# Attention scores of two heads on the two halves of TensorE's rows

## The chip, the core and the metric

The kernel runs on one core of a Trainium2 chip. The metric is the device time of one execution in microseconds. Before the change it is 956.52 us, the median of three runs (956.5 to 957.92).

## What is computed

A decoder trunk of two layers on a sequence of 512 tokens and 1024 channels: a pooling mixer and a squared-ReLU MLP, then stick-breaking attention and a second MLP, with RMSNorms around each. All data is float32. The change touches the attention, which has 16 heads of 64 channels:

```python
def stick_breaking_attention(q, k, v):
    for i in range(S // Q_BLOCK):            # blocks of 128 queries
        kv_len = (i + 1) * Q_BLOCK
        z = einsum('bhqd,bhkd->bhqk', q_blk, k_blk) * inv_sqrt_d
        mask = s_idx < t_idx
        log1m = where(mask, -softplus(z), 0.0)
        excl = cumsum(log1m, axis=3, reverse=True) - log1m
        a = where(mask, exp(log_sigmoid(z) + excl), 0.0)
        outs.append(einsum('bhqk,bhkd->bhqd', a, v_blk))
```

## The kernel before

**Precision.** Products of float32 values are made from rounded parts (type fp32r): every operand is split into a high part, a rounded copy made by ScalarE (ACT), and a low part, the rest, made by a subtraction on VectorE (DVE). A product is high x high + high x low + low x high. In most of the kernel these are three matmuls into one PSUM bank (`mm3`, `up_block`).

**Stages.** The pooling layer, the first MLP, the attention stage, the second MLP. The attention stage handles heads in eight pairs, since the 128 columns of one projection are two heads of 64. Its steps are written out in `ATT_ORDER`: P projects keys and queries of a pair (`queries_keys`, 48 matmuls), S makes its scores and weights (`weights`), T turns the weights by transposes (`transposed`, L1023, 20 per pair), A multiplies them with the values (`mix_pair`, L1040), V projects values and O projects the output. Between S and T of one pair stands the projection P of the next. A scheduler decides the final order within each engine from its own simulation, except for the last pair: there the steps are listed by hand in `END_ORDER` and keep that order on every engine ("z" are scores, "x" and "y" the two sigmoids, "sc" the scan, "mu" the product, "T" the transposes).

**Scores before.** Of a pair's projection, partitions 0 to 63 belong to head 0 and 64 to 127 to head 1. `queries_keys` gives each head tiles of its own. Its q tile has the high part on its own half of the partitions and the low part on the other half; its k tile has the high part on both halves. So one matmul over all 128 rows sums high x high and low x high. A third tile, `kl`, has the low part of k on the own half and zeros on the other (set once on POOL, L918), and a second matmul adds high x low. Per pair this takes six copies on ACT (L925, L926, L935) and four subtractions on DVE (L927, L936), each on 64 partitions and 512 columns.

`Head.scores` (L979, L980) makes the scores of one head in three PSUM banks: 128 queries against 512 keys, 128 against 384, and one bank with 128 against 256 twice. The last of these needs only 128 keys but is made 256 wide. That is 2 x 4 matmuls per head and 16 per pair.

**After the scores.** `against` (L988) writes sigmoid(-z) into `u`, and `for_` (L1000) writes sigmoid(z) into `w`, both on ACT. `scan` (L1004) is one DVE scan over all 1280 columns of a head; `weigh` (L1010) multiplies its result into `w`. Then `turn` transposes `w` on TensorE into PSUM, `high` (L1029, ACT) and `low` (L1033, DVE) split the transposed weights, and `products` multiplies them with the values.

PSUM has eight banks of 128 x 512, all from one pool (`ps`).

Of the kernel before, what the change touches and what calls it, by code (L numbers as in the profile page):

```python
# [10 lines left out]
F32 = mybir.dt.float32  # L11
F32R = mybir.dt.float32r
ACT = mybir.ActivationFunctionType
ALU = mybir.AluOpType

P = 128
# [16 lines left out]
TS = [slice(t * P, (t + 1) * P) for t in range(T)]  # L33
# [3 lines left out]
SEG = {3: (0, 512), 2: (512, 384), 1: (896, 256), 0: (1152, 128)}  # L37
# [33 lines left out]

END_ORDER = [
    (w if w.startswith("d7") else w.rstrip("0123456789"), [int(c) for c in w if c.isdigit() and not w.startswith("d7")])
    for w in """D6 R0 R1 z01 z00 x01 z02 x00 z11 x02 z12 y02 sc0 A60 y01 y00 x11 z10 oc60 A61 y11 x10 od60 E01 y10
    mu0 oc61 x12 E00 y12 od61 sc1 T00 hh6 T02 T01 ah00 O00 ah02 d7h ah01 O01 hl6 al02 F01 mu1 E11 ov01
    T11 al00 T10 ah11 al01 F11 ah10 al11 T12 A70 al10 ah12 d7l al12 ov00 A71 oc70 od70 O10 oc71 od71 F00
    ov10 hh7 O11 hl7 G01 ov11 G00 ev01 G11 ev00 s01 E10 ev11 s00 g01 s11 F10 V0 g00 G10 a01 O20 a00 S01
# [13 lines left out]
def trunk(ctx, tc, x, consts, grow, pw, wup, wdn, wq, wk, wv, wo, out):  # L91
    nc = tc.nc
# [11 lines left out]
    def name(s):  # L104
        uid[0] += 1
        return f"{s}{uid[0]}"

    def ps():
        return psum.tile([P, 512], F32, tag="ps", name=name("ps"))
# [29 lines left out]
    behind, latest = {}, {}  # L139
# [81 lines left out]
    def make():  # L221
        k, src, scaled = queue.pop(0)
        if k in kept:
            made[k] = place(k)
            for n, t in enumerate(made[k]):
                latest["sp"] = nc.sync.dma_start(t.bitcast(F32), kept[k][n])
            return
        made[k] = weight(src, place(k), scaled)

    def fill(n=1):  # L230
        if gate[0]:
            behind.update(latest)
        for _ in range(n):
            if queue and len(made) < ahead and (queue[0][0][0] != "dn" or dn_pool[0]):
                make()

    def get(key):
        while key not in made:
            make()
        return made.pop(key)  # L240

    for l in range(2):
        if l == 1:
            n = len(queue)
# [176 lines left out]
    def need(*tiles):  # L421
        for t in tiles:
            if t in pending:
                pending.pop(t).transpose()
# [67 lines left out]
    def y_tiles():  # L492
        return [work.tile([P, D], F32, tag=f"y{t}", name=name(f"y{t}")) for t in range(T)]
# [207 lines left out]
    def up_block(pu, w, cols):  # L701
        wh = w[0].rearrange("p (k c) -> p k c", k=KC)
        wl = w[1].rearrange("p (k c) -> p k c", k=KC)
        for k in range(KC):
            nc.tensor.matmul(pu[:, cols], wh[:, k, :], xnh[:, k, cols], start=k == 0, stop=False)  # L705
            nc.tensor.matmul(pu[:, cols], wh[:, k, :], xnl[:, k, cols], start=False, stop=False)  # L706
            nc.tensor.matmul(pu[:, cols], wl[:, k, :], xnh[:, k, cols], start=False, stop=k == KC - 1)  # L707


    with tc.tile_pool(name="mix0", bufs=1, reuse_waits="tile") as mp:  # L710
# [29 lines left out]
        left, stats, ups, ys, own = {}, {}, {}, {}, {}  # L740
# [128 lines left out]
    with tc.tile_pool(name="att", bufs=1, reuse_waits="tile") as ap:  # L869
# [30 lines left out]
        def project(key):  # L900
            need(*range(T))
            if key in started:
                pq, w = started.pop(key)
                up_block(pq, w, slice(S // 2, S))
            else:
                pq = ps()
                up_block(pq, get(key), slice(0, S))
            return pq

        def qk_tile(tag):  # L910
            return ap.tile([P, S], F32R, tag=tag, name=name(tag))

        half = [slice(0, HD), slice(HD, P)]


        kls = [qk_tile(f"kl{a}") for a in range(2)]
        for a in range(2):
            nc.gpsimd.memset(kls[a][half[1 - a], :].bitcast(F32), 0.0)  # L918

        def queries_keys(p):  # L920
            qs, ks = [], []
            pk = project(("k", p))
            for a in range(2):
                k, kl, own, other = qk_tile(f"k{a}"), kls[a], half[a], half[1 - a]
                nc.scalar.copy(k[own, :], pk[own, :])  # L925
                latest["act"] = nc.scalar.copy(k[other, :], pk[own, :])  # L926
                latest["dve"] = nc.vector.tensor_tensor(  # L927
                    out=kl[own, :], in0=pk[own, :], in1=k[own, :].bitcast(F32), op=ALU.subtract
                )
                ks.append(k)  # L930
            fill()
            pq = project(("q", p))
            for a in range(2):
                q, own, other = qk_tile(f"q{a}"), half[a], half[1 - a]
                latest["act"] = nc.scalar.copy(q[own, :], pq[own, :])  # L935
                latest["dve"] = nc.vector.tensor_tensor(  # L936
                    out=q[other, :], in0=pq[own, :], in1=q[own, :].bitcast(F32), op=ALU.subtract
                )
                qs.append(q)
            fill()  # L940
            return qs, ks

        begin = ap.tile([P, NSEG], mybir.dt.bfloat16, tag="begin", name="begin")
        nc.gpsimd.memset(begin, 0.0)
# [1 line left out]
        for lo, n in SEG.values():  # L949
# [3 lines left out]
                out=d, in_=d, pattern=[[-1, P + c]], base=c - 1, channel_multiplier=1,  # L953
# [6 lines left out]
        class Head:  # L960
# [9 lines left out]
                self.qk, self.p, self.a, self.u = qk, p, a, us[a]  # L970
                self.pz, self.pt, self.parts, self.to = {}, {}, {}, {}

            def scores(self, b):
                q, k, kl = self.qk[0][self.a], self.qk[1][self.a], kls[self.a]
                pz = self.pz[b] = ps()
                o = 0
                for i in self.SCORES[b][0]:
                    n = max(256, (i + 1) * P)
                    nc.tensor.matmul(pz[:, o : o + n], q[:, TS[i]], k[:, :n], start=True, stop=False)  # L979
                    nc.tensor.matmul(pz[:, o : o + n], q[:, TS[i]], kl[:, :n], start=False, stop=True)  # L980
                    o += n

            def against(self, b):
                tiles, at = self.SCORES[b]
# [64 lines left out]
            def out(self, o):  # L1049
                own = half[self.a]  # L1050
                nc.vector.tensor_tensor(out=o[own, :], in0=self.po[half[0], :], in1=o[own, :], op=ALU.add)

        def weights(p):
            hs = [Head(qk[p], p, a) for a in range(2)]
            for x in hs:
                for b in range(3):
                    x.scores(b)
                    x.against(b)
                    x.for_(b)
                x.scan()  # L1060
                x.weigh()
            return hs
# [27 lines left out]
        vs, os, wos, y = {}, {}, {}, y_tiles()  # L1090
# [6 lines left out]
        def end():  # L1097

            p, last = PAIRS - 2, PAIRS - 1
            heads[last] = [Head(qk[last], last, a) for a in range(2)]  # L1100
            w = {c: get(("o", c)) for c in range(2, 6)}
            bank, o, ups, up = {}, {}, {}, {}
# [66 lines left out]
            def half_up(j):  # L1169
# [2 lines left out]

            last_heads = heads[last]
            steps = {
                "z": lambda a, b: last_heads[a].scores(b), "x": lambda a, b: last_heads[a].against(b),
                "y": lambda a, b: last_heads[a].for_(b), "sc": lambda a: last_heads[a].scan(),
                "mu": lambda a: last_heads[a].weigh(), "T": lambda a, b: last_heads[a].turn(b),
                "ah": lambda a, b: last_heads[a].high(b), "al": lambda a, b: last_heads[a].low(b),
# [24 lines left out]
        for what, i, part in ATT_ORDER:  # L1203
            if what == "V":
                values(i, part)
            elif what == "K":
                start(("k", i))
            elif what == "P":
                qk[i] = queries_keys(i)
                if i == PAIRS - 1:  # L1210
                    until(("o", 5))
            elif what == "S":
                gate[0] = True
                heads[i] = weights(i)
                fill()
            elif what == "T":
                transposed(heads[i])
                behind.update(latest)
            elif what == "A":
                mix_pair(i, vs[i // 2][1])  # L1220
            elif what == "O" and part:
                out_proj(i, part)
                if i == 0:
                    with tc.issue_after(latest["sp"].ins):
                        gpost1 = gain_row(R_MIX_POST1)
            elif what == "E":
                end()
# [58 lines left out]
```

## Time and profile before

| | |
|---|---|
| median of three runs | 956.52 us (956.5 to 957.92) |
| profiled execution, span | 955.0 us |
| instructions | 12510 |
| TensorE matmuls (PE) busy | 940.7 us, 4757 of them |
| weight loads (PEld) busy | 799.6 us |
| VectorE (DVE) busy | 707.1 us |
| ScalarE (ACT) busy | 576.6 us |
| GpSimd (POOL) busy | 44.7 us |
| TensorE clock granted | 0.997 of full speed |

The profiled execution is one run beside the three timed ones; the profile gives its span from the first to the last instruction. In the profile, PE is the matmuls and PEld the weight loads, which overlap them. A group's row gives line, engine, operation, tiles written and read, shape and count, then busy microseconds and the mean nanoseconds of one, then idle time of the engine before it and what ended it. Matmuls are pipelined: one of 512 columns is shown with 0.39 us while the next starts sooner, so start-to-start times are what counts for TensorE. A row of the timeline is start, duration, engine, line, operation, tiles.

### The profile page before, as it was taken

The numbers are of one execution on the slowest core, as the hardware profiler recorded it, in microseconds if no ns is written. First come the engines' busy times: TensorE is split into PE (matmuls) and PEld (weight loads), VectorE is DVE, ScalarE is ACT, GpSimd is POOL, SyncE is SP. The second block draws the span as 40 slices with busy tenths as digits, with TensorE's granted clock in tenths as the row PEclk, the third lists the DMA queues.
The fourth block names the chain that finished last, engine by engine and source line by source line (L and its number), as shares of the span: only waits on it lengthen the run. The fifth ranks groups of instructions, "written<-read, shape, count | busy, mean of one in ns | idle before, by whom it ended". The sixth has DMA issues, their size and how long they took to land.

```text
span 955.0 us, 12510 instructions
## 1 busy us (share of the span) xinstructions
PE 940.7 (98%) x4757; PEld 799.6 (84%) x4758; DVE 707.1 (74%) x810; ACT 576.6 (60%) x1015; POOL 44.7 (5%) x88
## 2 busy tenths in 40 slices
PE   9999999999999999999999999999999999999996
PEld 6998888888888878999899988898888888888885
DVE  5875799988979866476577778874595966957856
ACT  6667979788775646456656554775545544444632
POOL 2300000000000004000000000300000000000002
PEclk9999999999999999999999999999999999999998
DMA  8244969789697750422434271342513233133102
GB/s 307 99 175 151 338 216 359 293 282 343 221 326 266 273 192 2 179 88 88 162 125 171 95 265 45 127 139 68 197 39 129 97 132 110 45 132 110 47 21 88
DMA packets 43261, 156.14 MB, mean 163 GB/s; under 512 B 4289, under 2 KB 4673, under 8 KB 43202
## 3 DMA queue, kind: packets, MB, share of 16 engines
q1 hardware_dynamic: 43202, 155.36, 45.4%
q8 instruction: 37, 0.61, 0.3%
q14 instruction: 22, 0.18, 0.1%
HBM read 121.79 MB, written 33.55 MB: 163 GB/s over the span
## 4 chain that ended last, share of the span: by engine, by line
PE 86%; DVE 4%; ACT 3%; POOL 3%; DMA 2%; issue 1%; SPq 0%; POOLq 0%; DVEq 0%; ACTq 0%
PE ps L587 27%; PE ps L707 15%; PE ps L705 15%; PE ps L706 15%; PE ps L284 2%; PE ps L285 2%; PE ps L286 2%; PE ps L1040 2%; ACT xn L269 2%; PE ps L819 1%; PE ps L1023 1%; POOL stat L273 1%; DVE x L333 1%; PE ps L979 1%; POOL stat L280 1%
## 5 line engine op out<-in xcount | busy, mean ns | idle before, releaser
L587 PE MATMUL ps<-w,a 128*128 128x512 f32 x1176 | 278.6, 389 | 0.0
L707 PE MATMUL ps<-xnh,w 128*128 128x512 f32 (+1 forms) x712 | 261.6, 368 | 0.1
L706 PE MATMUL ps<-xnl,w 128*128 128x512 f32 (+1 forms) x712 | 261.5, 368 | 0.0
L705 PE MATMUL ps<-xnh,w 128*128 128x512 f32 (+1 forms) x712 | 261.2, 368 | 0.0
L587 PEld LDWEIGHTS ps<-w,a 128*128 128x128 f32 x1176 | 220.7, 188 | 45.9 <-DVE w L266 0.2
L707 PEld LDWEIGHTS ps<-xnh,w 128*128 128x128 f32 x712 | 134.2, 188 | 22.4 <-DVE w L840 0.3
L706 PEld LDWEIGHTS ps<-xnl,w 128*128 128x128 f32 x712 | 134.2, 189 | 21.8
L705 PEld LDWEIGHTS ps<-xnh,w 128*128 128x128 f32 x712 | 133.7, 189 | 22.1
L596 DVE TENSOR_TENSOR y<-ps,y 128x512 f32<-128x512 f32 x124 | 84.4, 686 | 42.0 <-PE ps L587 41.8
L156 DVE TENSOR_TENSOR w<-raw,w 128x1024 fp32r<-128x1024 f32 x58 | 70.9, 1222 | 57.7 <-ACT w L154 57.5
L154 ACT CAST w<-raw 128x1024 fp32r<-128x1024 f32 x58 | 61.0, 1051 | 80.5 <-PE ps L707 80.5
L265 ACT CAST a<-r 128x768 fp32r<-128x768 f32 (+1 forms) x60 | 47.6, 794 | 72.4 <-PE ps L587 54.6
L266 DVE TENSOR_TENSOR a<-r,a 128x768 fp32r<-128x768 f32 (+1 forms) x60 | 54.0, 900 | 11.8 <-ACT a L265 11.6
L265 ACT CAST w<-e 128x1536 fp32r<-128x1536 f32 (+1 forms) x30 | 41.8, 1395 | 25.6 <-DVE e L561 16.2
L1004 DVE TENSOR_TENSOR_SCAN e<-u,begin 128x1280 f32<-128x1280 f32 x16 | 45.2, 2822 | 11.3 <-ACT u L988 10.4
L266 DVE TENSOR_TENSOR w<-e,w 128x1536 fp32r<-128x1536 f32 (+1 forms) x30 | 49.4, 1647 | 1.8 <-ACT w L265 1.6
L165 ACT ACTIVATE apart<-apart,eye 128x128 f32<-128x128 f32 (+1 forms) x132 | 43.1, 407 | 0.2 <-DMA apart<-in_wk 0.2
L266 DVE TENSOR_TENSOR w<-w,w 128x1536 fp32r<-128x1536 f32 (+1 forms) x20 | 33.0, 1649 | 8.1 <-ACT w L265 8.1
L619 ACT ACTIVATE r<-ps 128x512 f32<-128x512 f32 x56 | 33.0, 589 | 8.3 <-PE ps L707 8.2
L284 PE MATMUL ps<-w,xnh 128*128 128x256 f32 x128 | 36.6, 286 | 1.4 <-ACT xnh L395 1.4
L266 DVE TENSOR_TENSOR w<-xn,w 128x1536 fp32r<-128x1536 f32 (+1 forms) x20 | 33.0, 1650 | 5.6 <-ACT w L265 5.5
L620 ACT ACTIVATE r<-r 128x512 f32<-128x512 f32 x56 | 35.5, 633 | 1.3
(131 smaller groups left out, 1394.7 us busy)
## 6 DMA issues: line engine op xcount, KB each, us to landing
raw<-in_wup SPq DMA_DIRECT2D x64, 512.0 KB, 3.8
w<-kept SPq DMA_DIRECT2D x60, 512.0 KB, 4.1
kept<-wx SPq DMA_DIRECT2D x30, 512.0 KB, 4.9
w<-in_wdn SPq DMA_DIRECT2D x8, 1536.0 KB, 7.7
kept<-apart SPq DMA_DIRECT2D x24, 512.0 KB, 5.1
xn<-in_wdn SPq DMA_DIRECT2D x8, 1536.0 KB, 8.2
raw<-in_wdn SPq DMA_DIRECT2D x8, 512.0 KB, 3.5
apart<-in_wk SPq DMA_DIRECT2D x7, 512.0 KB, 6.4
```

Source lines behind the costliest of these rows:

```text
L154: nc.scalar.copy(hi, raw)
L156: nc.vector.tensor_tensor(out=lo, in0=raw, in1=hi.bitcast(F32), op=ALU.subtract)
L165: nc.scalar.mul(c, c, gc[:, lo + k : lo + k + 1])
L265: latest["act"] = nc.scalar.copy(hi, src)
L266: latest["dve"] = nc.vector.tensor_tensor(out=lo, in0=src, in1=hi.bitcast(F32), op=ALU.subtract)
L284: nc.tensor.matmul(dst, ah, bh, start=start, stop=False)
L587: nc.tensor.matmul(bank, a[:, x, q, TS[t]], w[:, z, q], start=start and q == 0 and k == 0, stop=q == self.n - 1 and k == 2, skip_group_che ...
L596: nc.vector.tensor_tensor(out=part, in0=bank, in1=part, op=ALU.add)
L705: nc.tensor.matmul(pu[:, cols], wh[:, k, :], xnh[:, k, cols], start=k == 0, stop=False)
L706: nc.tensor.matmul(pu[:, cols], wh[:, k, :], xnl[:, k, cols], start=False, stop=False)
L707: nc.tensor.matmul(pu[:, cols], wl[:, k, :], xnh[:, k, cols], start=False, stop=k == KC - 1)
L1004: nc.vector.tensor_tensor_scan(out=self.e[:, ::-1], data0=self.u[:, 1:][:, ::-1], data1=begin[:, ::-1], initial=0.0, op0=ALU.mult, op1=ALU ...
```

## The change

Both heads of a pair share four tiles: high and low of k, high and low of q, each over all 128 partitions. That takes two copies and two subtractions per pair, each on 128 partitions. Each score block is now three matmuls over 64 rows per head (high x high, high x low, low x high). The head on the lower half of the partitions uses rows 0 to 63 of the array, the other rows 64 to 127, and the matmuls of the two heads alternate. They write different PSUM banks. The last block is 128 wide. A pair has 24 score matmuls. The scores of both heads now come before the sigmoids in the program, bank by bank, and in the hand-written order of the last pair the steps z1, z0, z2 stand for both heads.

```diff
-    for w in """D6 R0 R1 z01 z00 x01 z02 x00 z11 x02 z12 y02 sc0 A60 y01 y00 x11 z10 oc60 A61 y11 x10 od60 E01 y10
+    for w in """D6 R0 R1 z1 z0 x01 z2 x00 x02 y02 sc0 A60 y01 y00 x11 oc60 A61 y11 x10 od60 E01 y10
...
-        kls = [qk_tile(f"kl{a}") for a in range(2)]
-        for a in range(2):
-            nc.gpsimd.memset(kls[a][half[1 - a], :].bitcast(F32), 0.0)
-
         def queries_keys(p):
-            qs, ks = [], []
-            pk = project(("k", p))
-            for a in range(2):
-                k, kl, own, other = qk_tile(f"k{a}"), kls[a], half[a], half[1 - a]
-                nc.scalar.copy(k[own, :], pk[own, :])
-                latest["act"] = nc.scalar.copy(k[other, :], pk[own, :])
-                latest["dve"] = nc.vector.tensor_tensor(
-                    out=kl[own, :], in0=pk[own, :], in1=k[own, :].bitcast(F32), op=ALU.subtract
-                )
-                ks.append(k)
-            fill()
-            pq = project(("q", p))
-            for a in range(2):
-                q, own, other = qk_tile(f"q{a}"), half[a], half[1 - a]
-                latest["act"] = nc.scalar.copy(q[own, :], pq[own, :])
-                latest["dve"] = nc.vector.tensor_tensor(
-                    out=q[other, :], in0=pq[own, :], in1=q[own, :].bitcast(F32), op=ALU.subtract
-                )
-                qs.append(q)
-            fill()
-            return qs, ks
+            both = []
+            for what in "kq":
+                src = project((what, p))
+                hi, lo = qk_tile(f"{what}h"), qk_tile(f"{what}l")
+                latest["act"] = nc.scalar.copy(hi, src)
+                latest["dve"] = nc.vector.tensor_tensor(out=lo, in0=src, in1=hi.bitcast(F32), op=ALU.subtract)
+                both.append((hi, lo))
+                fill()
+            return both
...
-            def scores(self, b):
-                q, k, kl = self.qk[0][self.a], self.qk[1][self.a], kls[self.a]
-                pz = self.pz[b] = ps()
-                o = 0
-                for i in self.SCORES[b][0]:
-                    n = max(256, (i + 1) * P)
-                    nc.tensor.matmul(pz[:, o : o + n], q[:, TS[i]], k[:, :n], start=True, stop=False)
-                    nc.tensor.matmul(pz[:, o : o + n], q[:, TS[i]], kl[:, :n], start=False, stop=True)
-                    o += n
...
+        def scores(hs, b):
+            (kh, kl), (qh, ql) = hs[0].qk
+            for x in hs:
+                x.pz[b] = ps()
+            o = 0
+            for i in Head.SCORES[b][0]:
+                n = SEG[i][1]
+                for m, (x, y) in enumerate(((qh, kh), (qh, kl), (ql, kh))):
+                    for h in hs:
+                        own = half[h.a]
+                        nc.tensor.matmul(
+                            h.pz[b][:, o : o + n], x[own, TS[i]], y[own, :n], start=m == 0, stop=m == 2,
+                        )
+                o += n
...
             hs = [Head(qk[p], p, a) for a in range(2)]
+            for b in range(3):
+                scores(hs, b)
             for x in hs:
                 for b in range(3):
-                    x.scores(b)
                     x.against(b)
                     x.for_(b)
...
-                "z": lambda a, b: last_heads[a].scores(b), "x": lambda a, b: last_heads[a].against(b),
+                "z": lambda b: scores(last_heads, b), "x": lambda a, b: last_heads[a].against(b),
```

## Prediction

> **What bounds the kernel now.** I read the page's totals first, then the attention stage (about 385 to 587 us) by windows and waits, then the timeline of single instructions inside it.
>
> ```profile
> span 955.0 us, 12510 instructions
> ...
> PE 940.7 (98%) x4757; PEld 799.6 (84%) x4758; DVE 707.1 (74%) x810; ACT 576.6 (60%) x1015; POOL 44.7 (5%) x88
> ```
>
> Matmul busy is modelled, so the 98% alone proves little. The window and the waits of the stage do:
>
> ```profile
> core 0: us, PE busy (x) PEld busy (x) DVE busy (x) ACT busy (x) POOL busy (x), PEclk, DMA share, GB/s
> 430.00:450.00 20.00, 20.00 (x132) 18.40 (x131) 12.30 (x17) 13.03 (x28) 0.00 (x0) 1.00 0.27 102
> ```
>
> ```profile
> PEld ps L979 <- PE ps L980: 0.6, 1, 0.6
> ...
> PE ps L979 <- DVE q L936: 0.4, 1, 0.4
> ```
>
> From 390 to 575 us these are the longest waits of the matmul side: one event, before the last pair's scores. DVE and ACT are busy for under two thirds of the window. So TensorE sets the time here, and a microsecond of scores saved or added moves the end by a microsecond, unless it is eaten at the few places where TensorE has almost caught up with VectorE. The span is one execution; the median of the three times, 956.52, is 1.5 us above it, and I add the change in span to the median.
>
> **The scores before.** The first pair, both heads, on TensorE (start, duration):
>
> ```profile
> 396.58 0.39 PE L979 MATMUL ps<-k,q 128*128 128x512 f32 x1
> 396.81 0.40 PE L980 MATMUL ps<-kl,q 128*128 128x512 f32 x1
> 397.04 0.34 PE L979 MATMUL ps<-k,q 128*128 128x384 f32 x1
> 397.22 0.34 PE L980 MATMUL ps<-kl,q 128*128 128x384 f32 x1
> 397.39 0.28 PE L979 MATMUL ps<-k,q 128*128 128x256 f32 x1
> 397.51 0.28 PE L980 MATMUL ps<-kl,q 128*128 128x256 f32 x1
> 397.62 0.28 PE L979 MATMUL ps<-k,q 128*128 128x256 f32 x1
> ...
> 399.14 0.40 PE L705 MATMUL ps<-xnh,w 128*128 128x512 f32 x1
> ```
>
> What counts is start to start: 0.23 us for 512 columns, 0.175 for 384, 0.12 for 256. Sixteen matmuls take 399.14 - 396.58 = 2.56 us; eight pairs, 20.5 us. That is all the change has to work on.
>
> **The scores after.** Twenty-four matmuls of 64 rows, alternately for the head on the lower and the upper rows; the built program does place them at rows 0 and 64. Nothing in this trace runs on half the rows, so three prices are unknown: whether two matmuls run at once, whether their weight loads do, and what a change between 128-row and 64-row matmuls costs. For a narrow matmul the nearest rows are the transposes of 128 columns:
>
> ```profile
> 410.20 2.18 PE ps L1023 x20
> ```
>
> ```profile
> L979 PEld LDWEIGHTS ps<-k,q 128*128 128x128 f32 x64 | 12.1, 188 | 1.4 <-PE ps L980 0.6 <-DVE al L1033 0.2
> ```
>
> Twenty take 2.18 us, 0.11 each. A load lasts 0.188 but the next may start 0.11 behind it: that, not the columns, is the floor of one load with its matmul.
>
> If the two halves overlap wholly, a pass over the four blocks costs 0.23 + 0.175 + 0.12 + 0.11 = 0.63, three passes 1.90 us: 0.66 less per pair. If matmuls overlap but loads queue, each block takes two loads, 0.22, at least: 3 x (0.23 + 3 x 0.22) = 2.67, 0.11 more. If nothing overlaps, 6 x 0.63 = 3.80, 1.24 more. I take full overlap: the loads of this trace already run under matmuls, so loading isn't tied to an idle array. (The same page, section "Packing small matmuls: row/col tiling", has matmuls of different row groups start about 4 ns apart and loads overlap in-flight matmuls where row groups differ; on two loads at once it is silent. No run here shows either yet.)
>
> **Changing the mode.** Bounds: nothing, as between the lines above, whose starts keep their pace from one tile to another; or the pipe must empty and then load. Emptying is a matmul's 0.39 less its 0.23, 0.16 us; one load's pace after it 0.11 to 0.12: 0.28. I take 0.2, nearer to emptying, since some of the load may hide. (The Trainium skill, "TensorEngine Tiling (Array Packing)", Key Properties, says that changing the tiling mode drains the engine: it speaks against this change, and by it s is 0.16 at least and the sum below +1.2 us at least. No row of this trace shows it.) Seven pairs have one stretch of scores, two changes each. The fifth pair's scores are interleaved with the value products of the pair before it, as before, in six stretches of 3, 3, 3, 3, 5 and 7: twelve changes, and half-filled passes that leave only 0.1 of its 0.66. With the price s: seven pairs 7 x (-0.66 + 2s), the fifth -0.1 + 12s. At s = 0.2: -1.8 and +2.3.
>
> **Copies.** Per pair ACT drops six half copies for two whole ones, DVE four half subtractions for two:
>
> ```profile
> L926 ACT CAST k<-ps 64x512 fp32r<-64x512 f32 x16 | 9.3, 581 | 0.2
> ...
> L936 DVE TENSOR_TENSOR q<-ps,q 64x512 fp32r<-64x512 f32 x16 | 11.0, 689 | 7.3 <-ACT q L935 7.0
> ```
>
> ```profile
> L1033 DVE TENSOR_TENSOR al<-ps,ah 128x512 fp32r<-128x512 f32 x32 | 20.6, 685 | 0.8 <-ACT ah L1029 0.5
> ...
> L1029 ACT CAST ah<-ps 128x512 fp32r<-128x512 f32 x32 | 17.3, 592 | 4.8 <-PE ps L1023 4.5
> ```
>
> A copy costs the same with 64 or 128 partitions: ACT saves 6 x 0.58 - 2 x 0.59 = 2.3 us, DVE 4 x 0.69 - 2 x 0.685 = 1.4 us per pair. Both lie under TensorE, so this is worth nothing except before the last pair:
>
> ```profile
> 565.57 0.59 ACT q L935
> 566.18 0.69 DVE q L936
> 566.90 1.62 DVE al L1033 x3
> 568.55 0.70 DVE q L936
> 569.39 0.41 PE ps L979
> ```
>
> The second half-subtraction of q stands behind three of the turned weights, and TensorE waits for it. One whole subtraction at 566.18 is over before the scores begin: -0.6 us. The POOL memsets that go are on an idle engine, at no gain.
>
> **A wait that is added.** The built order computes both heads' scores block by block, and ACT then takes head 0, head 1, head 0 and so on, where it finished head 0 first. Head 0's scan on DVE starts later, and head 1's weights with it. The third pair has least room:
>
> ```profile
> 445.27 0.60 ACT L988 ACTIVATE u<-ps 128x511 f32<-128x511 f32 x1
> 445.77 0.59 ACT L1000 ACTIVATE w<-ps 128x512 f32<-128x512 f32 x1
> 446.25 0.50 ACT L988 ACTIVATE u<-ps 128x383 f32<-128x383 f32 x1
> 446.61 0.51 ACT L1000 ACTIVATE w<-ps 128x384 f32<-128x384 f32 x1
> 446.99 0.59 ACT L988 ACTIVATE u<-ps 128x255 f32<-128x255 f32 x2
> 447.40 0.55 ACT L1000 ACTIVATE w<-ps 128x384 f32<-128x384 f32 x1
> 447.77 0.68 ACT L265 CAST ohl<-o 128x512 fp32r<-128x512 f32 x1
> 448.28 1.11 ACT L154 CAST w<-raw 128x1024 fp32r<-128x1024 f32 x1
> ```
>
> ```profile
> 447.60 2.82 DVE L1004 TENSOR_TENSOR_SCAN e<-u,begin 128x1280 f32<-128x1280 f32 x1 [1.64 <-ACT u L988]
> ...
> 450.93 1.48 DVE L1010 TENSOR_TENSOR w<-w,e 128x1280 f32<-128x1280 f32 x1
> 452.33 1.22 DVE L156 TENSOR_TENSOR w<-raw,w 128x1024 fp32r<-128x1024 f32 x1
> 453.47 2.81 DVE L1004 TENSOR_TENSOR_SCAN e<-u,begin 128x1280 f32<-128x1280 f32 x1
> 456.20 0.66 DVE L927 TENSOR_TENSOR kl<-ps,k 64x512 fp32r<-64x512 f32 x1
> 456.78 1.47 DVE L1010 TENSOR_TENSOR w<-w,e 128x1280 f32<-128x1280 f32 x1
> ```
>
> ```profile
> 457.98 2.35 PE L1023 MATMUL ps<-eye,w 128*128 128x128 f32 x20
> ```
>
> Now head 1's product is done at 458.3, and its ten transposes begin at 457.98 + 10 x 0.11 = 459.1. After, by the start-to-start times above: ACT starts at about 445.5 (head 0's first block is complete two passes later); four activations of the first block 2 x 0.98, the copy 0.51, the weight 0.95, the second block 2 x 0.74, head 0's last pair 0.59: head 0's scan starts at 451.0 instead of 447.6. DVE's built order is scan 2.73, product 1.40, kl 0.58, scan 2.73, a weight's low part 1.14, product 1.5: done at 461.1. TensorE reaches head 1's transposes at 459.1 - 0.66 + 2 x 0.2 = 458.8 and waits 2.3 us (2.7 at s = 0); behind these transposes stand the 48 matmuls of the first output projection, all held. The same reckoning leaves the first and the fifth pair room of under 1 us, the others more: no wait there.
>
> **Sum**: -1.8 + 2.3 - 0.6 + 2.3 = +2.2 us; as a function of s, -2.6 + 24s. Span 957.2, time 956.5 + 2.2 = 958.7.
>
> **Rivals.** *Loads queue* (matmuls overlap, loads of the two halves take turns): for it, the loads' 0.11 pace is the tightest in this trace and never beaten by a load with a matmul; against it, each load fills only half the rows. (The Trainium skill's section "LDWEIGHTS" of the page named first gives columns / 1.2 whatever the number of rows: 24 loads in turn would be 24 x 0.107 = 2.57 us a pair, nearly this rival's; the trace agrees at 128 rows with its 0.11.) The sum: 7 x (0.11 + 0.4) + 2.6 for the fifth pair + 1.5 for the wait - 0.5 = +7.2: 963.7. *No overlap at all* (so the change doesn't do what it says): 7 x 1.64 + 3.6 + 0.4 - 0.3 = +15.2: 971.7; with free mode changes +10.2: 966.7. *Free mode changes with full overlap*, the other side: s under 0.025, worth -2.6: 953.9; it turns faster than no change at s = 0.11. For it, no transition among today's matmuls costs anything; against it, all of them use the same 128 rows.
>
> **How the numbers follow.** Forecast (full overlap, s between 0.1 and 0.28, -0.2 to +4.1): 0.36. Loads queue: 0.30. No overlap: 0.13. Free mode changes: 0.18. Something else: 0.03. A measurement here tells 0.2%, 1.9 us. Faster by more takes s under 0.03: 0.18 with the rest. Within 1.9: the forecast up to s = 0.18 and a little of the others, 0.22. Slower: 0.60. The range runs from the free case, 954, to queued loads with s at 0.28 (+9.4, 966) and no overlap with free changes, 967; the dear end of no overlap is left out.
>
> **What would show it.** Right: start to start in the score lines of about 0.23, 0.175, 0.12 and 0.11 per two matmuls; a gap of about 0.2 us before the first and after the last score matmul of each pair; a wait of over 2 us at the third pair's transposes for the weights' product; no wait for q at the last pair. Queued loads would show as 0.22 per two matmuls at every width, no overlap as 0.11 to 0.23 per single matmul. I am wrong if the gaps at the stretches' ends are absent, or if TensorE waits elsewhere for over 1 us.

## The result, and the profile after

| | before | after |
|---|---|---|
| median of five runs | 956.95 us (956.5 to 957.92) | 961.4 us (960.0 to 961.52) |
| profiled execution, span | 955.0 us | 959.7 us |

After over before is 1.0042, with a 95% interval of 1.0029 to 1.0054: 4.5 us slower, where +2.2 was forecast. The totals of the page after (engine, busy us, share, count):

```profile
PE 944.4 (98%) x4821; PEld 799.2 (83%) x4822; DVE 695.1 (72%) x794; ACT 558.8 (58%) x983; POOL 43.9 (5%) x86
```

VectorE has 12 us less work than before and ScalarE 18, as the six half copies and four half subtractions per pair should give, and that buys no time except at the wait for q before the last pair. TensorE has 64 matmuls more. The waits of TensorE between 370 and 576 us show that it is no longer always the engine that ends last. First the longest of before, then all of after (who waits for whom, us in total, times, longest):

```profile
PE ps L284 <- ACT xnh L395: 1.4, 1, 1.4
```

```profile
PE ps L995 <- DVE w L982: 2.6, 1, 2.6
PE ps L995 <- ACT ah L1001: 0.8, 1, 0.8
PE ps L284 <- ACT xnh L395: 0.4, 1, 0.4
```

Two waits are new, both of the transposes (L995) for head 1's weights. One wait shrank from 1.4 to 0.4 us, and it lies ahead of the scores, at the first projection of the stage. The wait for q before the last pair is gone.

**The scores.** The second pair after, on TensorE:

```profile
417.12 0.28 PE L286 MATMUL ps<-w,xnl 128*128 128x256 f32 x1
417.33 0.49 PE L1037 MATMUL ps<-kh,qh 64*128 64x512 f32 x2
417.67 0.40 PE L1037 MATMUL ps<-kl,qh 64*128 64x512 f32 x2
417.90 0.40 PE L1037 MATMUL ps<-kh,ql 64*128 64x512 f32 x2
418.13 0.33 PE L1037 MATMUL ps<-kh,qh 64*128 64x384 f32 x2
418.31 0.34 PE L1037 MATMUL ps<-kl,qh 64*128 64x384 f32 x2
...
419.18 0.28 PE L1037 MATMUL ps<-kh,ql 64*128 64x128 f32 x2
419.39 0.50 PE L1012 MATMUL ps<-ah,v 128*128 128x512 f32 x1
419.73 0.39 PE L1012 MATMUL ps<-al,v 128*128 128x512 f32 x1
```

"x2" is a matmul of each head, drawn as one row because the second starts within the first. Start to start, two matmuls take 0.23 us at 512 columns (417.67 to 417.90), 0.18 at 384 (418.13 to 418.31) and 0.12 at 256: what one of 128 rows took. The loads keep up: the three products have 64 loads each, with means of 184 and 185 ns, where a 128-row load took 188 ns. One of the three rows:

```profile
L1037 PEld LDWEIGHTS ps<-kl,qh 64*128 64x128 f32 x64 | 7.4, 185 | 0.3
```

The first matmul of a stretch is 0.34 from the next instead of 0.23, and the first 128-row matmul behind it (419.39) again 0.34. The last matmul ahead of each change is 0.21 from its successor (417.12 to 417.33, 419.18 to 419.39), where the pace is 0.12 and 0.11. So a change of mode costs 0.2 us, half on either side of it. Behind a stretch that ends in a 128-wide matmul, some 0.06 us of this belongs to the narrow matmul: in the kernel before with its last block 128 wide (`b3_no_padding`, below), where no mode changes, the 512-wide matmul behind a 128-wide one is 0.29 from its successor (398.53 to 398.82).

**The fifth pair**, whose scores alternate with the value products (L1012) of the pair before:

```profile
498.76 0.49 PE L1037 MATMUL ps<-kh,qh 64*128 64x512 f32 x1
499.10 0.39 PE L1037 MATMUL ps<-kl,qh 64*128 64x512 f32 x1
499.33 0.39 PE L1037 MATMUL ps<-kh,ql 64*128 64x512 f32 x1
499.65 0.44 PE L1012 MATMUL ps<-al,v 128*128 128x384 f32 x1
499.93 0.28 PE L1012 MATMUL ps<-ah,v 128*128 128x256 f32 x1
```

Here a stretch is the three matmuls of one block of one head. No "x2" stands in these rows: the other head's matmuls come in the next stretch.

**The third pair's transposes.** VectorE, then TensorE, then the same time by windows (window and its us, then busy us and count of PE, PEld, DVE, ACT and POOL, then TensorE's granted clock):

```profile
450.02 2.83 DVE L976 TENSOR_TENSOR_SCAN e<-u,begin 128x1280 f32<-128x1280 f32 x1 [0.75 <-ACT u L960]
...
457.69 1.20 DVE L156 TENSOR_TENSOR w<-raw,w 128x1024 fp32r<-128x1024 f32 x1
458.81 1.48 DVE L982 TENSOR_TENSOR w<-w,e 128x1280 f32<-128x1280 f32 x1
```

```profile
456.58 1.25 PE L995 MATMUL ps<-eye,w 128*128 128x128 f32 x10
460.44 2.37 PE L995 MATMUL ps<-eye,w 128*128 128x128 f32 x10 [2.61 <-DVE w L982]
462.46 0.78 PE L284 MATMUL ps<-w,ohl 128*128 128x512 f32 x1
```

```profile
456.60:460.00 3.40, 1.23 (x11) 0.99 (x9) 3.40 (x3) 1.84 (x4) 0.00 (x0) 1.00 0.67 220
460.00:463.40 3.40, 2.96 (x12) 2.86 (x13) 3.33 (x7) 1.45 (x3) 0.00 (x0) 0.50 0.23 90
463.40:465.00 1.60, 1.60 (x8) 1.27 (x7) 0.71 (x2) 0.42 (x1) 0.00 (x0) 0.99 0.00 0
```

Head 1's product (L982) starts at 458.81 and the last ten transposes at 460.44, 2.6 us after the ten before them ended. In the window of 460.0 to 463.4 the granted clock is 0.50: ten transposes take 2.02 us to the next matmul instead of 1.05, and the first matmuls of the output projection are stretched too.

The two traces from the first row of a step to the first row of the next, with 0.1 us or so that a stretch puts on its neighbours counted to it:

| step | measured | forecast |
|---|---|---|
| scores of pairs 1 to 4 and 6, each | -0.29 to -0.33 | -0.26 |
| scores of pair 7 | 0.0 | -0.26 |
| scores of the last pair, with the wait for q | -0.7 | -0.26 - 0.6 |
| fifth pair, scores and products | +3.3 | +2.3 |
| first pair's transposes | +1.0 | 0 |
| third pair's transposes and what follows | +3.9 | +2.3 |
| ahead of the first scores | -1.35 | 0 |
| sum | +4.6 | +2.2 |

The spans differ by 4.7.

### The profile page after: what moved, and what is told of

The parts are those of the page before. It is cut to its first block, busy times and chain, and to the rows that moved or that the text cites. A ratio compares the mean times of both kernels' runs of the same rounds, so it can differ in the third digit from the quotient of the medians.

```text
span 959.7 us, 12570 instructions
## 1 busy us (share of the span) xinstructions
PE 944.4 (98%) x4821; PEld 799.2 (83%) x4822; DVE 695.1 (72%) x794; ACT 558.8 (58%) x983; POOL 43.9 (5%) x86
## 4 chain that ended last, share of the span: by engine, by line
PE 88%; DVE 4%; ACT 3%; POOL 3%; issue 1%; DMA 1%; POOLq 0%; DVEq 0%; SPq 0%; ACTq 0%
PE ps L587 27%; PE ps L705 15%; PE ps L707 14%; PE ps L706 14%; PE ps L285 3%; PE ps L284 3%; PE ps L286 2%; PE ps L1012 2%; PE ps L1037 2%; PE ps L995 2%; ACT xn L269 2%; PE ps L819 1%; POOL stat L273 1%; DVE x L333 1%; POOL stat L280 1%
## 5 line engine op out<-in xcount | busy, mean ns | idle before, releaser
L156 DVE TENSOR_TENSOR w<-raw,w 128x1024 fp32r<-128x1024 f32 x58 | 70.8, 1221 | 57.9 <-ACT w L154 57.8
L286 PE MATMUL ps<-w,xnl 128*128 128x256 f32 x128 | 36.3, 283 | 0.0
```

The lines of the kernel that those rows point to most:

```text
L156: nc.vector.tensor_tensor(out=lo, in0=raw, in1=hi.bitcast(F32), op=ALU.subtract)
L286: nc.tensor.matmul(dst, al, bh, start=False, stop=stop)
```

## The experiments

Each was compared with the kernel before on the same chip; a change of time below is the median against 961.4 (after) or against the 956.7 to 956.8 that the kernel before had beside it.

**Head 0's sigmoids ahead of head 1's** (`e1_head0_first`). Theory: the two waits come from the order on ScalarE alone. Rival: they come from the scores ending sooner.

```diff
-                nc.scalar.activation(self.w[:, at : at + n], self.pz[b][:, :n], ACT.Sigmoid, scale=0.125)
+                self.done = nc.scalar.activation(self.w[:, at : at + n], self.pz[b][:, :n], ACT.Sigmoid, scale=0.125)
...
-                for b in range(3):
-                    x.against(b)
-                    x.for_(b)
+                with tc.issue_after(hs[0].done.ins) if x is hs[1] else nullcontext():
+                    for b in range(3):
+                        x.against(b)
+                        x.for_(b)
```

> The changed kernel with one order put back: ACT makes all seven sigmoids of head 0 before those of head 1; the scores stay as changed. If the waits at the transposes of the first and the third pair (blocks 1.0 and 3.8 us longer than before, the half clock behind the second included) come from ACT's alternation, both go and the time falls by about 4.8 us from 961.4 to 956.6. If DVE's load or PSUM banks make these waits, they stay and the time stays near 961.

Measured: 956.68 us (956.14 to 958.81, 11 runs), ratio 1.0001 (0.9993 to 1.001), 4.7 less than after. VectorE and TensorE at the third pair:

```profile
449.72 2.82 DVE L976 TENSOR_TENSOR_SCAN e<-u,begin 128x1280 f32<-128x1280 f32 x1
...
457.57 1.48 DVE L982 TENSOR_TENSOR w<-w,e 128x1280 f32<-128x1280 f32 x1
```

```profile
458.02 2.46 PE L995 MATMUL ps<-eye,w 128*128 128x128 f32 x20
```

Head 0's scan (first row) starts 4.77 us after the pair's first score matmul (444.95) instead of 6.51 (443.51 in after). With the time won the scheduler also put the product ahead of the second output weight's low part (L156), 1.14 us. All twenty transposes stand in one row, without a wait, and so it is at the first pair. By the table above the two places cost 1.0 and 3.9 us, and 4.7 are won back.

**The fourth pair's scores ahead of the third pair's products** (`e2_scores_before_products`), so that the scheduler doesn't interleave scores and products at the fifth pair (counting pairs from one).

```diff
-    ... V201 T3 A3
-    S4 P5 T4 V223 ...
+    ... V201 T3 S4
+    A3 P5 T4 V223 ...
```

> The changed kernel with the fifth pair's scores listed before the value products of the pair before it, so that its 24 score matmuls stand in one stretch: 2 mode changes there instead of 12. If a change costs 0.2 us and a broken pass is half lost, the stretch of scores and products falls from 8.4 us to about 4.7, and some 0.5 us of waiting for PSUM comes back: about -3, 958.3. If the interleaving only filled a wait for the turned weights, the time stays within 1 us of 961.4.

Measured: 958.62 us (956.69 to 959.73, 11 runs), ratio 1.0017 (1.0008 to 1.0026), 2.8 less than after. The 24 matmuls are one stretch of 2.41 us. The wait at the third pair is unchanged, 2.6 us, and a low clock comes with it. Here it begins only when TensorE already works again (the transposes restart at 460.68); a window behind them, columns as above:

```profile
462.60:463.60 1.00, 1.00 (x4) 0.81 (x3) 1.00 (x3) 0.15 (x1) 0.00 (x0) 0.50 0.00 0
```

**The same order in the kernel before** (`b2_scores_before_products`), to see whether the order by itself is worth anything.

> The kernel before, with the fifth pair's scores listed before the value products of the pair before it. Matmuls over all rows have no mode to change, so its interleaving costs nothing: 956.95, within 0.5. If the order itself is worth something (the rival for the kernel with that edit), it falls by over 1 us.

Measured: 956.91 us (956.02 to 958.51, 11 runs), ratio 1.0004 (0.9995 to 1.0013). It isn't: the 2.8 us are paid only where scores and products need different modes.

**Both edits** (`e3_both`).

> Both edits, head 0's sigmoids first and the fifth pair's scores in one stretch. If the two losses are separate they add: 961.4 - 4.8 - 3.1 = 953.5, faster than the kernel before (956.95) by about 0.35%. If one hides the other, or the waits move elsewhere, 956 to 957.

Measured: 953.62 us (952.96 to 955.24, 6 runs), ratio 0.9969 (0.9957 to 0.998): 7.8 us less than after, and faster than the kernel before. No wait of TensorE is left between 390 and 575 us.

**One head after the other** (`e4_heads_in_turn`), on the kernel with both edits: the same 24 matmuls of 64 rows, but all of head 0 first, so that the halves of the array can hardly meet.

```diff
-            for b in range(3):
-                scores(hs, b)
+            for x in hs:
+                for b in range(3):
+                    scores([x], b)
```

> As the kernel with both edits, but the score matmuls of head 0 all come before those of head 1, so that matmuls on the two halves of the rows hardly meet. If the halves overlap fully in the changed kernel, each pair's scores grow from 2.1 to about 3.9 us, 1.24 us or somewhat more each: 953.5 + 10 = 963.5. If what the alternation brings is small, 954 to 956.

Measured: 962.69 us (962.39 to 964.46, 5 runs), ratio 1.0064 (1.005 to 1.0078), 9.1 more than with both heads in turn. The second pair:

```profile
419.15 0.49 PE L1037 MATMUL ps<-kh,qh 64*128 64x512 f32 x1
419.48 0.39 PE L1037 MATMUL ps<-kl,qh 64*128 64x512 f32 x1
419.71 0.40 PE L1037 MATMUL ps<-kh,ql 64*128 64x512 f32 x1
...
422.78 0.50 PE L1012 MATMUL ps<-ah,v 128*128 128x512 f32 x1
```

A single matmul of 64 rows keeps the pace of one of 128, 0.23 and 0.17 us; the pair takes 422.78 - 419.15 = 3.63 us instead of 2.07. That is what the overlap is worth, 1.56 us a pair. At the first and the last pair the two heads still met in part.

**A shorter wait** (`e5_shorter_wait`): the changed kernel, with the low part of the second output weight queued behind head 1's product of the third pair, which should make the wait 1.1 us shorter (lines from L980 on have numbers higher by two). It asks whether the low clock follows from the length of the wait.

```diff
+        if k == ("o", 1):
+            behind["dve"] = weighed[5]
         made[k] = weight(src, place(k), scaled)
...
-                nc.vector.tensor_tensor(out=self.w, in0=self.w, in1=self.e, op=ALU.mult)
+                weighed.append(nc.vector.tensor_tensor(out=self.w, in0=self.w, in1=self.e, op=ALU.mult))
```

> The changed kernel with one DVE instruction moved: the low part of the second output weight (1.1 us) is queued behind head 1's product of the third pair instead of ahead of it. The wait at that pair's transposes shrinks from about 2.8 us to 1.7. If the half clock after it is the effect of the idle time, it goes too: -1.1 - 1.4 = -2.5, 958.9, with a granted clock of 1.00 throughout. If the half clock comes from something else it stays, and the time is 960.3.

Measured: 959.39 us (959.09 to 961.61, 5 runs), ratio 1.0035 (1.0022 to 1.0047), 2.0 less than after: more than the 1.0 us by which the wait shrank. TensorE, and the window behind the wait:

```profile
459.59 1.28 PE L997 MATMUL ps<-eye,w 128*128 128x128 f32 x10 [1.62 <-DVE w L984]
```

```profile
459.50:461.50 2.00, 1.91 (x14) 1.80 (x15) 2.00 (x3) 1.19 (x3) 0.00 (x0) 1.00 0.66 264
```

The wait is 1.62 us and the clock stays at 1.00. So at this place the low clock goes with the longer wait. One execution of each was profiled; the last section looks at what decides it.

**The padded block** (`b3_no_padding`): the kernel before with its last block 128 wide, as the changed kernel has it.

```diff
-                    n = max(256, (i + 1) * P)
+                    n = (i + 1) * P
```

> The kernel before with its last score block 128 columns wide instead of 256, as the changed kernel has it. A narrow matmul is bound by the load's pace of 0.11 us instead of 0.12, 32 of them: -0.3 us, not to be told from none. If narrow matmuls of this type run slower, +1 or more.

Measured: 956.79 us (956.14 to 958.46, 10 runs), ratio 0.9999 (0.999 to 1.0008). In the trace the stretch of a pair falls from 2.57 to 2.49 us, eight times 0.08; that is 0.6 us at most and not seen in the time.

**What makes the lead ahead of the first scores.** The changed kernel reaches them 1.35 us sooner. A first theory was an order on ScalarE, where a copy of v had moved behind the squares of x (`b1_square_order`, the kernel before with that order):

```diff
-                nc.scalar.copy(v[:, s, :, 0, :], pv4)
+                with tc.issue_after(latest["squares"].ins) if (u, s) == (0, 1) else nullcontext():
+                    nc.scalar.copy(v[:, s, :, 0, :], pv4)
```

> The kernel before with one ACT instruction moved, as the changed kernel has it: the copy of the second block of values goes behind both halves of the last squares of x at the end of the first MLP, instead of between them. If this is why the changed kernel reaches its first scores 1.35 us sooner, the time falls by 1.4 to 955.5. If that lead has another cause, it stays at 956.95.

Measured: 956.67 us (956.06 to 958.57, 11 runs), ratio 1.0 (0.9991 to 1.0009). That theory fell. GpSimd's queue shows another, before and after:

```profile
371.28 1.10 POOL L918 MEMSET kl<- 64x512 f32 x2
...
373.82 0.75 POOL L273 TENSOR_SCALAR stat<-stat,eps 128x1 f32<-128x1 f32 x1
374.53 1.03 POOL L952 TENSOR_SCALAR_AFFINE_SELECT begin<-begin 128x129 bf16<-128x129 bf16 x4
375.53 0.57 POOL L280 TENSOR_TENSOR stat<-stat,mhalf 128x1 f32<-128x1 f32 x1
```

```profile
372.26 1.03 POOL L933 TENSOR_SCALAR_AFFINE_SELECT begin<-begin 128x129 bf16<-128x129 bf16 x4
373.35 0.86 POOL L273 TENSOR_SCALAR stat<-stat,eps 128x1 f32<-128x1 f32 x1
374.30 0.57 POOL L280 TENSOR_TENSOR stat<-stat,mhalf 128x1 f32<-128x1 f32 x1
```

L273 adds up the mean square of a row tile (128 of the 512 tokens) and L280 takes its power of -1/2. L273 and the L280 behind it (the last row of each view) are the norm of the last row tile, whose normed values (xnh is their high part) the first projection of the stage needs. Before, the two memsets of the low keys (L918) stand ahead of them, and the affine selects of the scan's set-up lie between the two. After, the memsets are gone and the set-up is over when the sum starts. `b4_memsets_later` is the kernel before with the memsets issued behind that norm:

```diff
-            nc.gpsimd.memset(kls[a][half[1 - a], :].bitcast(F32), 0.0)
+            with tc.issue_after(latest["pool"].ins):
+                nc.gpsimd.memset(kls[a][half[1 - a], :].bitcast(F32), 0.0)
```

> The kernel before with the two memsets that zero the unused halves of the low keys issued behind the last row tile's last power on GpSimd, instead of ahead of that row tile's norm. Theory that these two memsets (0.52 us each) stood on the chain to the first attention matmuls, and that their going is why the changed kernel reaches its first scores over 1 us sooner: 956.95 - 1.1 = 955.8 us, the last power of that row tile ending about 1.1 us sooner and TensorE reaching its first scores at about 395.4 us of the span instead of 396.6. Rival, that GpSimd is idle there and the lead has another cause: 956.9 us, no change.

Measured: 955.87 us (955.31 to 956.19, 11 runs), ratio 0.999 (0.9982 to 0.9999), 0.9 less. GpSimd and TensorE's wait at the first projection:

```profile
374.13 0.87 POOL L273 TENSOR_SCALAR stat<-stat,eps 128x1 f32<-128x1 f32 x1
375.08 0.57 POOL L280 TENSOR_TENSOR stat<-stat,mhalf 128x1 f32<-128x1 f32 x1
```

```profile
380.85 0.39 PE L284 MATMUL ps<-w,xnh 128*128 128x256 f32 x1 [0.38 <-ACT xnh L395]
```

Take as a mark the start of the power of the row tile ahead of this one (370.66 in before, 371.09 here, 370.30 in after). From it to the end of the last power it is 5.4 us in before and 4.6 here and in after; TensorE waits 1.45 us, 0.38 and 0.36. From the mark to the first scores it is 1.08 us less here than in before, and 0.99 less in after. So 1.0 of the lead of 1.35 comes from the memsets, and by the remaining 0.36 the trace of after is ahead at the mark already; starts of one kernel's executions differ by as much.

**The rest of the set-up moved too** (`e6_both_setup_later`): the kernel with both edits, with all of GpSimd's set-up for the scan behind that norm.

> The changed kernel with head 0's sigmoids ahead of head 1's and the fourth pair's scores ahead of the third pair's products, and with GpSimd's whole set-up for the scan (the memset of the segment starts, 1.10 us, its affine selects, 1.03 us, and the memsets of the segment columns) issued behind the last row tile's last power. Theory that this set-up stands on the same chain: up to 1.0 us less, the share of the affine selects that lies between that row tile's sum and its power, so 952.6 us against the 953.6 of the two edits alone. Rival, that the chain ends there in something else once the memsets of the low keys are gone: 953.6 us.

Measured: 953.5 us (952.96 to 954.85, 6 runs), ratio 0.9966 (0.9954 to 0.9978), not to be told from 953.62. GpSimd now waits itself:

```profile
373.93 0.87 POOL L273 TENSOR_SCALAR stat<-stat,eps 128x1 f32<-128x1 f32 x1 [2.48 <-ACT xn L269]
```

The sum waits for ScalarE's squares, and its power ends 4.55 us after the same mark: without the memsets the set-up was no longer what ended last.

## Why the prediction was right, and where not

The sign, the range and most of the mechanism held; the forecast of 958.7 was 2.7 us low, of which 0.4 is the base (956.95 with five runs for 956.52 with three). By its steps:

- **Full overlap, of the matmuls and of their loads**: right. The pace per two matmuls is the forecast one, a pair's stretch 2.06 to 2.08 us for 1.90 and half of two changes, and the one-head-at-a-time kernel is 9.1 us slower. *Loads queue* fell: it needed 0.22 us per two loads where the rows show 0.11 to 0.12. *No overlap at all* fell with it. On this the Trainium skill ("TensorEngine Tiling (Array Packing)", Key Properties) says that tiles can load and multiply in parallel; the trace agrees, with two 64-row loads per 0.12 us. The page of the Trainium skill that the prediction calls "the same page" and "the page named first" is "TensorE: Matmul & The Clock Gate"; the 2.57 us a pair worked out from its section "LDWEIGHTS" for loads in turn did not come about. In the trace behind the rows of the second pair, the two matmuls of a row with "x2" start 2 to 6 ns apart and their two loads 2 to 7 ns apart (417.33 to 418.31): the loads of the two halves don't take turns, and the 4 ns between matmuls that the prediction gives from that page agree.
- **s = 0.2 for a change of mode**: right, 0.10 before and 0.10 behind the change. *Free mode changes*, the case on the faster side, fell by this, and by the two waits. The same Key Properties' rule that a change of mode drains the engine agrees with the direction; the page has no price, and the rows give it.
- **The fifth pair, +2.3**: measured +3.3. The price per change held there too: the row 498.76 is 0.34 from the next, and the product behind it (499.65) is 0.28 from its successor where it was 0.17 before. What failed is the other term, "half-filled passes that leave only 0.1 of its 0.66". A stretch of three is one head alone, so nothing overlaps in it: without the changes the six stretches are 2 x 3 x 0.23 + 2 x 3 x 0.175 + 1.17 (the last two, 0.72 + 0.84, less the changes in them) = 3.6 us, 0.9 more than the 2.7 of before instead of 0.1 less. Twelve changes at 0.2 on top make the +3.3.
- **The wait at the third pair, 2.3 us**: right in place, releaser and size (2.6). Missing was what a wait of that length does to the clock: it is 0.97 us more on the ten transposes, and 0.4 on the projection behind them (11.72 us, against 11.29 in the kernel with head 0 first).
- **"Room of under 1 us" at the first pair, so "no wait there"**: wrong by 1.0 us. VectorE, then TensorE there:

```profile
408.74 1.48 DVE L982 TENSOR_TENSOR w<-w,e 128x1280 f32<-128x1280 f32 x1
```

```profile
410.37 1.28 PE L995 MATMUL ps<-eye,w 128*128 128x128 f32 x10 [0.80 <-ACT ah L1001]
```

  The profile puts the wait down to ScalarE's copies ah, which end at 410.35. But the product ends at 410.22, 0.15 us ahead of the transposes, just as at the third pair (460.29 and 460.44), and I take it for the releaser. Counted from the pair's first score matmul, TensorE comes 0.4 us sooner than in before and the product ends 3.1 us later (in before it ended at 408.43, 2.7 us ahead of its transposes). Two parts of this were not in the reckoning: the third pass of head 0's first block stands behind other blocks in the built order, so that ScalarE starts 1.6 us after the first score matmul instead of 0.7, and VectorE takes a subtraction of k (0.6) ahead of the product.
- **Copies worth nothing except 0.6 before the last pair**: right. The wait for q is gone and the stretch there is 0.7 us shorter.
- **"The POOL memsets that go are on an idle engine, at no gain"**: wrong by 1.0 us in the kernel's favour (0.9 in the time of `b4_memsets_later`). GpSimd is busy 5% of the span, but for these 5 us it is the engine on the chain. The row that tells it, TensorE's wait of 1.4 us for xnh, lay outside the 390 to 575 us that were read for waits. (Of the waits inside, the prediction's "longest" left out one of 0.5 us, of weight loads for `al`; no matmul waited there.)
- Measured less forecast is +1.0 for the fifth pair, +1.0 and +1.6 for the two waits and -1.35 ahead of the scores: they cancelled in part, so it is luck that the forecast came nearer than its terms.
- The scores of pair 7 gained nothing, 0.3 us less than forecast, for the reason of the fifth pair: the heads are one block out of step. Its stretch of 2.41 us, first and last rows of the narrow blocks:

```profile
550.13 0.28 PE L1037 MATMUL ps<-kh,qh 64*128 64x256 f32 x1
550.25 0.28 PE L1037 MATMUL ps<-kl,qh 64*128 64x256 f32 x1
...
551.00 0.27 PE L1037 MATMUL ps<-kh,ql 64*128 64x128 f32 x1
```

  Three matmuls of 256 columns of one head run alone at 0.12 us each, and at the end three of 128 of the other ("x1"): some 0.35 us more than two by two. What puts the heads out of step was not tested. The one stretch of 2.41 us at the fifth pair in `e2_scores_before_products` has the same rows.
- One sum of the prediction is off, that of queued loads at s = 0.28: its own terms give +9.1 to +9.3 instead of +9.4, which leaves the bound of 966 as it is.

The change as such is worth 2.3 us less than before, once its scores stand in one stretch and ScalarE finishes one head first: 953.6 against the 955.9 of the kernel before with its memsets moved (each measured beside the kernel before, at 956.7 and 956.8). What made it slower was the order that came with it.

## What to carry to other kernels

Two matmuls on the two halves of the array's rows cost as much as one, but only while both are there: before counting on it, read in the built order whether every stretch holds both, and put 0.2 us on each change of mode (two per stretch). When a change merges two producers' work, ask in which order the next engine takes it: the consumer that needed one of them first will wait, and its longest wait may bring a low clock with it. An engine that is busy 5% of the time can still be the one that ends last for a few microseconds; read the waits from where its work stands, not only the stage that is edited.

## What the runs showed of the hardware beyond that

After TensorE's 2.6 us of idleness its granted clock was 0.50 for 3.41 us, in both kernels with that wait; after 1.6 us, at the same place, it wasn't. The start lies 2.2 us into the wait in one (460.02) and 1.3 us behind its end in the other (462.00). The Trainium skill ("TensorE: Matmul & The Clock Gate", "HAM oscillation") puts the limit at gaps of about 3.4 us; these rows show less being enough. The Trainium skill's section "What's actually happening" of that page has a free-running window of 3413 ns, which agrees with the length seen and with the wandering start.

The same was seen once more at a place that no edit touches, the first down-projection of the first MLP, in the profiled executions of two kernels (head 0 first, and one head after the other). By windows, columns as above: head 0 first, then the kernel before with its memsets moved, then the kernel with the shorter wait.

```profile
346.34:349.75 3.41, 1.49 (x5) 1.04 (x6) 1.48 (x2) 2.09 (x2) 0.00 (x0) 1.00 0.20 82
349.75:353.16 3.41, 3.41 (x9) 2.66 (x9) 0.97 (x1) 0.00 (x0) 0.00 (x0) 0.50 0.68 232
```

```profile
344.63:348.05 3.42, 2.17 (x9) 1.24 (x7) 1.36 (x3) 1.05 (x1) 0.00 (x0) 1.00 0.66 217
```

```profile
456.60:460.01 3.41, 1.79 (x16) 1.49 (x15) 3.38 (x3) 1.84 (x4) 0.00 (x0) 1.00 0.56 215
```

At the down-projection TensorE is idle for 1.3 and 0.8 us with one matmul between in the first of the two kernels, for 1.2 and 0.8 us in the second, and in most others for less; the one before with its memsets moved idles for 1.2 and 0.8 us there and keeps its clock, so length alone doesn't decide. The traces show what goes with it. In each of the four with such a low stretch, its start and the fall at the kernel's end, where TensorE has no work left, lie a whole number of 3.413 us apart (in after, 954.95 - 460.02 = 494.93 us, 145 times). Counted back from the fall at the end, the other traces can be divided into the same intervals. Ahead of the four low stretches TensorE was busy for 1.23, 1.32, 1.49 and 1.56 us of an interval's 3.41. In all twelve traces every interval at full clock with 1.56 us of work or less was followed by a low clock, and none with 1.78 or more. With the memsets moved, the boundary at 348.05 parts the two idle times, which leaves 2.17 us of work in the interval; the shorter wait lies in one interval and leaves 1.79. So in these traces the clock falls where an interval holds less than about half of work. That is read off the rows; no run varied it alone.

Where the boundaries fall differs from trace to trace (460.02 and 462.00 above, at the same wait), so the low clock is in part a matter of chance. Of the eleven executions of `e2_scores_before_products`, nine have a mean granted clock of 0.994 to 0.996 and take 958.1 to 959.7 us; two have 0.998 and take 956.7 and 957.5. At the down-projection the profiled execution with the low clock is about 2 us longer than the median of its kernel: 958.81 beside 956.68 with head 0 first, 964.46 beside 962.69 with one head after the other.
